# A hybrid decoder block on one core: every tile that TensorE reads begins at the same address modulo 256 bytes

## The chip, the cores and the metric

One core of one Trainium2 chip runs the whole block in one program. The metric is the device time of one execution in microseconds (us). The core has TensorE (PE), which multiplies a stationary tile of up to 128 x 128, loaded ahead as weights, by a moving tile of up to 512 columns; VectorE (DVE), ScalarE (ACT) and GpSimd (POOL) for the elementwise work; and SyncE (SP), which issues most of the DMAs. SBUF holds the tiles, as one line of bytes in each of 128 partitions. An address here is the byte in that line at which a tile begins, and its class is that address modulo 256.

## The reference

1024 tokens of 1024 features in float32; 256 memory tokens.

```python
h = rmsnorm(x, g_mix_norm)
proj = jnp.einsum('bsd,de->bse', h, w_in)
sb_q, sb_k, sb_v, fx_q, fx_k, fx_v, f_logit, m_q, gate_logit = split_columns(proj, SPLITS)
o_sb = stick_breaking_attention(...)      # 8 heads of 64, strictly causal
o_fox = forgetting_attention(...)         # 8 heads of 64, causal softmax with decay
o_mem = memory_attention(...)             # 4 heads of 128 over 256 memory tokens
gates = jax.nn.sigmoid(gate_logit.reshape(b, s, N_BRANCH, D_MODEL))
merged = gates[:, :, 0] * br_sb + gates[:, :, 1] * br_fox + gates[:, :, 2] * br_mem
x = x + jnp.einsum('bsd,de->bse', merged, w_out)
h2 = rmsnorm(x, g_mlp_norm)
u = jax.nn.relu(jnp.einsum('bsd,df->bsf', h2, w_ff_up))      # 1024 -> 4096
x = x + jnp.einsum('bsf,fd->bsd', u * u, w_ff_down)          # 4096 -> 1024
```

Each `br_` is one attention's output times its 512 x 1024 branch matrix.

## The kernel before, in words

**Precision.** A float32 operand is split into a high and a low half in the type fp32r: ACT copies the raw tile into the high half, and DVE subtracts this from the raw tile into the low half (L1056 and L1057, L141 and L142, L1976 and L1977). A product is three matmuls into one PSUM bank: high by high, high by low, low by high. The function `mm3` (L145, matmuls at L149 to L151) shows it; other stages write the same three out (L1146, L1458, L1983, L2225, L2663). The large products of 1024 x 1024 and up are made as seven half-size products of sums and differences (P1 to P7) in place of eight.

**Stages**, in us of the profiled span: norms and transposes of the tokens (L467), value and key projections and the memory's (L1146) up to 116; the query and key projections in seven products (L1458) up to 485, whose middle, 195 to 365, has the tokens stationary and 256 columns of weights moving, and whose rest has the weights stationary and 512 columns of tokens moving; attention (transposes L919, scores L936, sums and outputs L825 to L872) up to 880, with the gates and two of the three branches (L1146) laid between; more of L1146 up to 921; the last branch (`last_branch`, L149 to L151) up to 966; the output projection (L2225) up to 1049; the MLP up (L1983) up to 1366; the MLP down (L2663) to the end.

**Order.** From the start to the end of attention, and again in the MLP up, a small planner in the kernel lays down the order of each engine from costs and due times. The last branch and what follows it are written as plain loops, and there the tile framework puts the instructions of each engine in order, from its model of when tiles come free.

**Memory.** A pool gives each tag so many buffers, and the framework places pools from the left, or with side="right" from the right end. Tiles of one tag take its buffers in turn; a new tile waits until the old one's readers are done.
- `C` (L85): small statistics tiles (`st`, 27 of 32 bytes), `sm`, the identity `ident` for transposes, `fn`.
- `W` (L308): two `raw` tiles and three pairs `whi`, `wlo` for weights in float32 and fp32r, of WS = 4 x 264 floats, so 4224 bytes each, which is 16.5 times 256: neighbours alternate between two classes. `load_w` (L132) and the planner (`WP`, `RAW`, L356 and L357) take them, and `wtile` and `right_tiles` (L1863, L1866) reuse them as right-hand operands of the output projection.
- Right side: `EDGE` (L303), a pad of 24 floats, then `RA` (the transposed tokens `hTh`, `hTl`, later `x`), `E`, `MT`, and later `RB`.
- Left working tiles behind `W`: `R`, `N`, then `A` (L1608: `h`, `v`, `e`, `r` and the mask `later`), `A2` (`pth`, `ptl`, `ob`, `es`, `o`), in the MLP `M` (`raw`, `oh`, `ol`, `cu`), in the last branch `G` (`gt`, `tmp`).

**The last branch** takes four column groups of weights `ws[d2]`. Some are loaded ahead, the others in the loop by `load_w`, each with two gates rows `gt` of 128 x 1024; it also splits the right operand of the first product P1 of the output projection (`right_tiles("P1")`, at d2 == 3). Per half-row: three matmuls for each k into a bank, then DVE multiplies by the gate into `tmp` and adds it to `g`, and for the first halves ACT and DVE make the high and low half (`oh`, `ol`).

Of the kernel before, what the change touches and what calls it, by code (L numbers as in the profile page):

```python
# [14 lines left out]
F32 = mybir.dt.float32  # L15
F32R = mybir.dt.float32r
I32 = mybir.dt.int32
AF = mybir.ActivationFunctionType
# [3 lines left out]
P = 128  # L22
# [9 lines left out]
WS = 4 * 264  # L32
# [11 lines left out]
def tile_hybrid_block(  # L44
# [20 lines left out]
    nc = tc.nc  # L65
# [16 lines left out]
        def close(self):  # L82
            self.cm.__exit__(None, None, None)

    C = Pool("c", st=27, ss=4)  # L85
    dram = ctx.enter_context(tc.tile_pool(name="dram", bufs=1, space=bass.MemoryType.DRAM))
    psum = ctx.enter_context(tc.tile_pool(name="ps", bufs=1, space=bass.MemoryType.PSUM))
    PSB = {"pp": 3, "sc": 2, "tr": 2, "pv": 1}
# [9 lines left out]
        return bank(ROT[flip[0] % 5])  # L98


    ident = C.p.tile([P, P], F32, tag="ident", name="ident")
    make_identity(nc, ident)
    sm = C.p.tile([P, 8], F32, tag="sm", name="sm")
    zero, one = sm[:, 0:1], sm[:, 1:2]
    nc.vector.memset(zero, 0.0)
    nc.vector.memset(one, 1.0)
# [1 line left out]
    nc.vector.memset(eps, EPS * 2.0 ** (2 / 3))  # L108

    def root_table():  # L110
        nc.scalar.activation(C.t("st", [P, 8])[:, :1], one, AF.Sqrt)
    root_table()
    o_scr = [dram.tile([512, S], F32, name=f"o_scr{b}", tag=f"o_scr{b}") for b in range(3)]
    low_scr = dram.tile([512, S], F32, name="low_scr", tag="low_scr")
# [14 lines left out]
    def stat(n, dt=F32):  # L129
        return C.t("st", [P, 8], dt)[:, :n]  # L130

    def load_w(pieces, kk, n, pool=None):  # L132

        pool = pool or W
        raw = W.t("raw", [P, WS])[:, :kk * n].rearrange("p (k n) -> p k n", n=n)
        for off, src in pieces:
            m = src.shape[1]
            nc.sync.dma_start(raw[:, :, off:off + m], src.rearrange("(k p) n -> p k n", p=P))
        hi = pool.t("whi", [P, WS], F32R)[:, :kk * n].rearrange("p (k n) -> p k n", n=n)
        lo = pool.t("wlo", [P, WS], F32R)[:, :kk * n].rearrange("p (k n) -> p k n", n=n)  # L140
        nc.scalar.activation(hi, raw, AF.Copy)  # L141
        nc.vector.tensor_tensor(lo, raw, f32(hi), ALU.subtract)  # L142
        return hi, lo
# [156 lines left out]
        yield Sleep(machine.pipe + 2.0 - machine.now)  # L300


    EDGE = Pool("edge", side="right", edge=1)  # L303
    EDGE.t("edge", [P, 24])
    RA = Pool("ra", side="right", h=4, g0=1, g1=1, g2=1, g3=1)
    E = Pool("e", side="right", sn=10)
    MT = Pool("mt", side="right", mt=4)
    W = Pool("w", raw=2, whi=3, wlo=3)  # L308
    R = Pool("r", raw=4, s1=1)
    N = Pool("n0", gb=2, xt=7, xj=1)  # L310

# [28 lines left out]
    fox_order = (2, 3, 0, 1)  # L340
    fn = C.p.tile([P, 64], F32, tag="fn", name="fn")

# [6 lines left out]
    def tiles(pool, tag, n, shape, dt=F32):  # L349
        return Places([pool.t(tag, [P, shape], dt) for _ in range(n)])  # L350

    PP, SC, TR, PV = (banks(tag) for tag in ("pp", "sc", "tr", "pv"))
    ES, OO, EL, RR, HT, PH, PL, OB, VV, BK, LATER, NONE, RQ = (Places([]) for _ in range(13))
    SN, RS, S1 = tiles(E, "sn", 10, 512), tiles(R, "raw", 4, 1024), R.t("s1", [P, 4, 256])
    XT = tiles(N, "xt", 7, D)
    WP = Places([(W.t("whi", [P, WS], F32R), W.t("wlo", [P, WS], F32R)) for _ in range(3)])  # L356
    RAW = tiles(W, "raw", 2, WS)  # L357

    def passes(a, b):
        return ((a[0], b[0]), (a[0], b[1]), (a[1], b[0]))  # L360
# [719 lines left out]
    def loader(tasks):  # L1080
        while tasks:
# [15 lines left out]
            for load in t.loads:  # L1097
                raw, first = ahead.pop(0) if ahead else (None, False)
                pair = yield Get(WP)
                _, kk, n = load  # L1100
# [498 lines left out]
    def second_part():  # L1599
        def opened(name, *tags):  # L1600
            pool = holder[name] = Pool(name, **{tag: n for _, tag, n, _, _ in tags})
            for place, tag, n, shape, dt in tags:
# [3 lines left out]
        holder["T"].close()  # L1606
        R.close()
        opened("A", (HT, "h", 12, 512, F32R), (VV, "v", 2, 2048, F32R), (EL, "e", 4, D, F32), (RR, "r", 3, D, F32),  # L1608
               (LATER, "later", 1, 544, F32))
        later = holder["later"] = LATER.free[0][:, :513]  # L1610
        halves = [RR.free.popleft() for _ in range(2)]
        RQ.put(*(t[:, i * 512:(i + 1) * 512] for t in halves for i in range(2)))
# [248 lines left out]
    left, right, ring = {}, {}, {}  # L1861

    def wtile(tag, dt):  # L1863
        return W.t(tag, [P, WS], dt)[:, :1024].rearrange("p (k n) -> p k n", k=2)

    def right_tiles(kind):  # L1866

# [5 lines left out]
    def last_branch(gpool, os_, ws):  # L1873
        b = order[2][0]
        for d2 in range(4):
# [7 lines left out]
            for dd in range(2):  # L1883
# [9 lines left out]
                if d == 7:  # L1893
                    nc.scalar.activation(C.t("st", [P, 8])[:, :1], gt[:, :1], AF.Sqrt, bias=one, scale=0.0)
                for half in range(2):
# [53 lines left out]
    for s in range(0, ST, 2):  # L1949
        t = RA.t("h", [P, 2, D])  # L1950
        xm += [t[:, 0, :], t[:, 1, :]]

    hb = {}
# [8 lines left out]
    raws, ops, pieces = {}, {}, {}  # L1962
# [48 lines left out]
    def free(what=None):  # L2011
# [6 lines left out]
        else:  # L2018
            sb[0].close()
            M.close()  # L2020
            W.close()
            RB.close()
# [675 lines left out]
        XR.close()  # L2698

    RA.close()  # L2700
    EDGE.close()
    C.close()


# [22 lines left out]
```

## Time and profile before

| what | value |
| --- | --- |
| runs of before | 1678.10, 1678.14, 1678.90 us; median 1678.14 |
| the profiled execution | 1677.32 us, of which the span of the trace is 1675.5 |
| instructions | 24,997, of which 9118 matmuls |
| DMA | 284.32 MB, mean 170 GB/s |

The span begins with the first instruction and ends with the last; the profiled execution's own time is 1.8 us more. A matmul's start is recorded, its end modelled, so that the difference of two starts is the pace, and a duration is the pace and some 0.16 us. L is the line of the kernel before, and the operands of a matmul stand as out<-moving,stationary, so that pp<-h,whi has the tile h moving and the weights' high half stationary. In its form, 128*128 is the stationary tile and 128x512 the moving one.

### The profile page before, as it was taken

How to read it: one execution, taken by the hardware profiler on the slowest of the kernel's cores; microseconds unless marked ns; L12 is line 12 of the kernel's file. 1: busy time of each engine (PE TensorE's matmuls, PEld its weight loads, DVE VectorE, ACT ScalarE, POOL GpSimd, SP SyncE). 2: the span in 40 equal slices, each digit the busy share in tenths (PEclk: the TensorE clock that was granted, in tenths of full speed). 3: DMA queues.
4: the chain of work that ended last, by engine and by line, in shares of the span. 5: the costliest groups of instructions: out<-in, count | busy, mean ns of one | idle time of the engine just before them, and what ended most of it. 6: DMA issues, size and time to landing. Idle time of an engine off the chain costs nothing.

```text
span 1675.5 us, 24997 instructions
## 1 busy us (share of the span) xinstructions
PE 1665.9 (99%) x9118; PEld 1432.9 (86%) x9118; DVE 1292.2 (77%) x2079; ACT 849.0 (51%) x1474; POOL 255.2 (15%) x440
## 2 busy tenths in 40 slices
PE   9999999999999999999999999999999999999999
PEld 9998899998888888888888887878888888888887
DVE  7967678855449888878877898987777776787875
ACT  6445555535458898876771446533233235333331
POOL 0001000000153132255400011021221120000000
PEclk9999999999999999999999999999999999999999
DMA  6445434467374455477747552144444375464532
GB/s 246 150 159 170 163 109 147 138 187 253 130 245 133 148 156 164 138 228 220 241 142 222 206 182 95 56 155 154 144 154 154 142 274 218 176 209 174 201 126 76
DMA packets 142221, 284.32 MB, mean 170 GB/s; under 512 B 16913, under 2 KB 53329, under 8 KB 142098
## 3 DMA queue, kind: packets, MB, share of 16 engines
q1 hardware_dynamic: 110562, 183.08, 32.0%
q0 software_dynamic: 31536, 99.64, 19.0%
q8 instruction: 72, 1.18, 0.3%
q14 instruction: 51, 0.42, 0.1%
HBM read 189.83 MB, written 92.83 MB: 169 GB/s over the span
## 4 chain that ended last, share of the span: by engine, by line
PE 91%; DVE 4%; ACT 1%; issue 1%; DMA 0%; DVEq 0%; ACTq 0%
PE pp L1458 11%; PE pp L1983 10%; PE pp L1146 9%; PE pp L2663 8%; PE sc L1458 7%; PE sc L1146 6%; PE sc L1983 5%; PE tr L2663 4%; PE sc L2663 4%; PE tr L919 4%; PE pv L1458 3%; PE pv L2663 3%; PE tr L1983 2%; PE sc L936 2%; PE pp L936 2%; DVE h L1919 1%
## 5 line engine op out<-in xcount | busy, mean ns | idle before, releaser
L1057 DVE TENSOR_TENSOR wlo<-raw,whi 128x1024 fp32r<-128x1024 f32 (+1 forms) x88 | 107.4, 1221 | 80.6 <-ACT whi L1056 80.2
L1056 ACT ACTIVATE whi<-raw 128x1024 fp32r<-128x1024 f32 (+1 forms) x88 | 93.2, 1059 | 79.0 <-PE pp L1458 32.7
L1983 PE MATMUL pp<-h,oh 128*128 128x512 f32 x384 | 120.6, 395 | 0.7 <-ACT cu L2068 0.6
L926 DVE TENSOR_TENSOR ptl<-tr,pth 128x512 fp32r<-128x512 f32 (+1 forms) x160 | 99.0, 627 | 24.1 <-ACT pth L924 23.3
L924 ACT ACTIVATE pth<-tr 128x512 fp32r<-128x512 f32 (+1 forms) x160 | 87.4, 557 | 34.5 <-PE sc L936 15.4
L1983 PEld LDWEIGHTS pp<-h,oh 128*128 128x128 f32 x384 | 72.1, 188 | 18.4 <-ACT cu L2068 1.5
L1375 POOL DMA_DIRECT2D raw<-w_in x32 | 24.1, 754 | 396.6 <-DVE wlo L1057 396.6
L1458 PE MATMUL pp<-h,whi 128*128 128x512 f32 x248 | 77.7, 394 | 0.0
L1146 PE MATMUL sc<-h,whi 128*128 128x512 f32 (+1 forms) x254 | 77.2, 387 | 0.0
L1983 PE MATMUL pp<-h,ol 128*128 128x512 f32 x192 | 75.8, 395 | 0.0
L1458 PE MATMUL pp<-whi,h 128*128 128x256 f32 x384 | 72.1, 283 | 0.0
L845 DVE TENSOR_TENSOR_SCAN e<-r,e 128x384 f32<-128x384 f32 (+3 forms) x64 | 66.3, 1043 | 7.0 <-ACT e L830 6.6
L1976 ACT ACTIVATE oh<-raw 128x512 fp32r<-128x512 f32 x64 | 39.4, 624 | 61.9 <-DVE raw L1919 61.9
L2663 PE MATMUL pp<-h,h 128*128 128x512 f32 x288 | 66.6, 389 | 0.0
L2663 PE MATMUL pp<-sop,sop 128*128 128x512 f32 x288 | 66.6, 389 | 0.0
L2663 PEld LDWEIGHTS pp<-h,h 128*128 128x128 f32 x288 | 54.1, 188 | 11.3
L2663 PEld LDWEIGHTS pp<-sop,sop 128*128 128x128 f32 x288 | 54.1, 188 | 11.3
L919 PE MATMUL tr<-ident,e 128*128 128x128 f32 x416 | 62.5, 273 | 0.0
L1458 PEld LDWEIGHTS pp<-whi,h 128*128 128x128 f32 x384 | 60.4, 189 | 0.0
L919 PEld LDWEIGHTS tr<-ident,e 128*128 128x128 f32 x416 | 50.6, 140 | 10.0
L1977 DVE TENSOR_TENSOR ol<-raw,oh 128x512 fp32r<-128x512 f32 x64 | 43.1, 688 | 16.8 <-ACT oh L1976 16.8
L1458 PEld LDWEIGHTS pp<-h,whi 128*128 128x128 f32 x248 | 46.7, 189 | 11.0
(562 smaller groups left out, 5193.9 us busy)
## 6 DMA issues: line engine op xcount, KB each, us to landing
ur<-s_scr SPq DMA_DIRECT2D x26, 1024.0 KB
raw<-w_in POOLq DMA_DIRECT2D x42, 512.0 KB, 5.0
raw<-w_up SPq DMA_DIRECT2D x60, 256.0 KB
s_scr<-s POOLq DMA_DIRECT2D x60, 256.0 KB, 2.6
g<-w_down SPq DMA_DIRECT2D x14, 1024.0 KB
s_scr<-cu POOLq DMA_DIRECT2D x48, 256.0 KB, 2.8
h<-sbk_scr POOLq DMA_DIRECT2D x64, 128.0 KB, 3.1
o<-gate_scr SPq DMA_DIRECT2D x32, 256.0 KB
```

Of the source, the lines that this page charges most:

```text
L845: nc.vector.tensor_tensor_scan(out=back, data0=rho[:, :u][:, ::-1], data1=back, initial=0.0 if last else beta[:, c + u:c + u + 1], op0=ALU ...
L919: nc.tensor.transpose(tr[:, jj * 256 + a * P:jj * 256 + (a + 1) * P], es[a][:, j * P:(j + 1) * P], ident)
L924: yield Op("ACT", act_time(512 - lo_c), lambda: nc.scalar.activation(ph[:, lo_c:], tr[:, lo_c:], AF.Copy))
L926: yield Op("DVE", dve_time(512 - lo_c), lambda: nc.vector.tensor_tensor(pl[:, lo_c:], tr[:, lo_c:], f32(ph[:, lo_c:]), ALU.subtract))
L936: nc.tensor.matmul(pv[0][:, c_:256], pair.v[:, j, b, :], p_[:, jj * 256 + c_:(jj + 1) * 256], start=(k == 0 and n_ == 0 and i == 0), stop= ...
L1056: yield Op("ACT", 0.03 + act_time(m), lambda: nc.scalar.activation(hi, raw, AF.Copy))
L1057: yield Op("DVE", dve_time(m), lambda: nc.vector.tensor_tensor(lo, raw, f32(hi), ALU.subtract))
L1146: nc.tensor.matmul(ps, a_, b_, start=(first and i == 0), stop=(last and i == n - 1))
L1458: nc.tensor.matmul(out_, a_, b_, start=(first and n == 0 and j == 0), stop=(last and n == 3 and j == len(todo) - 1), skip_group_check=True)
L1977: nc.vector.tensor_tensor(l_, src, f32(h_), ALU.subtract)
L1983: nc.tensor.matmul(ps, w[a_][:, k * P:(k + 1) * P], h[b_][k], start=(first and k == 0 and i == 0), stop=(last and k == 3 and i == 2), skip ...
L2663: nc.tensor.matmul(ps, a_[:, c, qs], b_[:, c, :], start=(kind in ("P1", "P2", "P7") and c == 0 and i == 0), stop=(kind in ("P2", "P4", "P3 ...
```

## The change

All tiles that TensorE reads get an address that is 224 modulo 256. The type of each instruction, its shape and its count stay.

| tiles | class before | class after |
| --- | --- | --- |
| `ident` | 128 | 224 |
| the three pairs, high / low half | 0 / 128, 128 / 0, 0 / 128 | 224 / 224 |
| `raw` tiles of `W` | 0, 128 | 96, used as operands from column 32 on: 224 |
| left working tiles (`h`, `v`, `e`, `oh`, `ol`, `cu`, ... and the MLP-down tiles `sop`, `ur`) | 0 | 224 |
| `pth`, `ptl`, `ob`, behind the mask | 128 | 224 |
| right side (`hTh`, `hTl`, `mt`, `sn`, `x`, `RB`) | 128 | 224 |

In the MLP down the operands made in the right-side tiles (`h`) are all of class 128 before, those made in the left ones (`sop`) all of class 0, and the two do not meet in one step.

- `C`: one `st` tile less (26), a `warm` tile for the table load, `sm` and `warm` ahead of `ident`.
- `W`: eight slots of their own (`SLOTS`, `ROOM`) in the order ha, ra, la, rb, hb, lb, hc, lc, of 4224, 4096 (hb, lb) and 4352 bytes (hc, lc), taken in turn by `wide`; before, three `whi`, three `wlo` and two `raw` buffers of one size. The turns go by the count of calls, so that the calls past the planner may find another slot than before.
- `EDGE` goes; `later` has 576 floats in place of 544 (its first 513 are used).

```diff
--- before.py
+++ after.py
@@ -82,7 +82,7 @@
         def close(self):
             self.cm.__exit__(None, None, None)
 
-    C = Pool("c", st=27, ss=4)
+    C = Pool("c", st=26, ss=4)
     dram = ctx.enter_context(tc.tile_pool(name="dram", bufs=1, space=bass.MemoryType.DRAM))
     psum = ctx.enter_context(tc.tile_pool(name="ps", bufs=1, space=bass.MemoryType.PSUM))
     PSB = {"pp": 3, "sc": 2, "tr": 2, "pv": 1}
@@ -98,9 +98,10 @@
         return bank(ROT[flip[0] % 5])
 
 
+    sm = C.p.tile([P, 8], F32, tag="sm", name="sm")
+    warm = C.t("st", [P, 8])
     ident = C.p.tile([P, P], F32, tag="ident", name="ident")
     make_identity(nc, ident)
-    sm = C.p.tile([P, 8], F32, tag="sm", name="sm")
     zero, one = sm[:, 0:1], sm[:, 1:2]
     nc.vector.memset(zero, 0.0)
     nc.vector.memset(one, 1.0)
@@ -108,7 +109,7 @@
     nc.vector.memset(eps, EPS * 2.0 ** (2 / 3))
 
     def root_table():
-        nc.scalar.activation(C.t("st", [P, 8])[:, :1], one, AF.Sqrt)
+        nc.scalar.activation(warm[:, :1], one, AF.Sqrt)
     root_table()
     o_scr = [dram.tile([512, S], F32, name=f"o_scr{b}", tag=f"o_scr{b}") for b in range(3)]
     low_scr = dram.tile([512, S], F32, name="low_scr", tag="low_scr")
@@ -129,15 +130,14 @@
     def stat(n, dt=F32):
         return C.t("st", [P, 8], dt)[:, :n]
 
-    def load_w(pieces, kk, n, pool=None):
-
-        pool = pool or W
-        raw = W.t("raw", [P, WS])[:, :kk * n].rearrange("p (k n) -> p k n", n=n)
+    def load_w(pieces, kk, n):
+
+        raw = wide("raw")[:, :kk * n].rearrange("p (k n) -> p k n", n=n)
         for off, src in pieces:
             m = src.shape[1]
             nc.sync.dma_start(raw[:, :, off:off + m], src.rearrange("(k p) n -> p k n", p=P))
-        hi = pool.t("whi", [P, WS], F32R)[:, :kk * n].rearrange("p (k n) -> p k n", n=n)
-        lo = pool.t("wlo", [P, WS], F32R)[:, :kk * n].rearrange("p (k n) -> p k n", n=n)
+        hi = wide("whi", F32R)[:, :kk * n].rearrange("p (k n) -> p k n", n=n)
+        lo = wide("wlo", F32R)[:, :kk * n].rearrange("p (k n) -> p k n", n=n)
         nc.scalar.activation(hi, raw, AF.Copy)
         nc.vector.tensor_tensor(lo, raw, f32(hi), ALU.subtract)
         return hi, lo
@@ -300,12 +300,18 @@
         yield Sleep(machine.pipe + 2.0 - machine.now)
 
 
-    EDGE = Pool("edge", side="right", edge=1)
-    EDGE.t("edge", [P, 24])
     RA = Pool("ra", side="right", h=4, g0=1, g1=1, g2=1, g3=1)
     E = Pool("e", side="right", sn=10)
     MT = Pool("mt", side="right", mt=4)
-    W = Pool("w", raw=2, whi=3, wlo=3)
+    SLOTS = {"whi": ("ha", "hb", "hc"), "wlo": ("la", "lb", "lc"), "raw": ("ra", "rb")}
+    ROOM = {"ha": WS, "ra": WS, "la": WS, "rb": WS, "hb": 1024, "lb": 1024, "hc": WS + 32, "lc": WS + 32}
+    W = Pool("w", **{slot: 1 for slot in ROOM})
+    taken = dict.fromkeys(SLOTS, 0)
+
+    def wide(tag, dt=F32):
+        slot = SLOTS[tag][taken[tag] % len(SLOTS[tag])]
+        taken[tag] += 1
+        return W.t(slot, [P, ROOM[slot]], dt)
     R = Pool("r", raw=4, s1=1)
     N = Pool("n0", gb=2, xt=7, xj=1)
 
@@ -353,8 +359,10 @@
     ES, OO, EL, RR, HT, PH, PL, OB, VV, BK, LATER, NONE, RQ = (Places([]) for _ in range(13))
     SN, RS, S1 = tiles(E, "sn", 10, 512), tiles(R, "raw", 4, 1024), R.t("s1", [P, 4, 256])
     XT = tiles(N, "xt", 7, D)
-    WP = Places([(W.t("whi", [P, WS], F32R), W.t("wlo", [P, WS], F32R)) for _ in range(3)])
-    RAW = tiles(W, "raw", 2, WS)
+    made_w = {tag: [] for tag in SLOTS}
+    for tag in ("whi", "raw", "wlo", "raw", "whi", "wlo", "whi", "wlo"):
+        made_w[tag].append(wide(tag, F32 if tag == "raw" else F32R))
+    WP, RAW = Places(list(zip(made_w["whi"], made_w["wlo"]))), Places(made_w["raw"])
 
     def passes(a, b):
         return ((a[0], b[0]), (a[0], b[1]), (a[1], b[0]))
@@ -1606,7 +1614,7 @@
         holder["T"].close()
         R.close()
         opened("A", (HT, "h", 12, 512, F32R), (VV, "v", 2, 2048, F32R), (EL, "e", 4, D, F32), (RR, "r", 3, D, F32),
-               (LATER, "later", 1, 544, F32))
+               (LATER, "later", 1, 576, F32))
         later = holder["later"] = LATER.free[0][:, :513]
         halves = [RR.free.popleft() for _ in range(2)]
         RQ.put(*(t[:, i * 512:(i + 1) * 512] for t in halves for i in range(2)))
@@ -1861,7 +1869,8 @@
     left, right, ring = {}, {}, {}
 
     def wtile(tag, dt):
-        return W.t(tag, [P, WS], dt)[:, :1024].rearrange("p (k n) -> p k n", k=2)
+        t = wide(tag, dt)
+        return (t[:, 32:WS] if tag == "raw" else t[:, :1024]).rearrange("p (k n) -> p k n", k=2)
 
     def right_tiles(kind):
 
@@ -2698,7 +2707,6 @@
         XR.close()
 
     RA.close()
-    EDGE.close()
     C.close()
```

On PE and POOL the instructions stand in the order of before. On ACT, DVE and SP they stand in another order in the last branch, where the weights of the third and fourth column groups now take another slot in turn.

ACT in the last branch, before: `gt` are sigmoids of the gates, `oh` high halves of the sum `g`, `whi415` the high half of the fourth weights, `whi417` that of the right operand of P1.

```order
L1892 ACTIVATE gt381_9293<-gt381_9293 128x1024
L1892 ACTIVATE gt386_9330<-gt386_9330 128x1024
L1905 ACTIVATE oh357_9269<-g0301_7470 128x512
L1905 ACTIVATE oh358_9270<-g0301_7470 128x512
L1892 ACTIVATE gt391_9368<-gt391_9368 128x1024
L1905 ACTIVATE oh359_9271<-g1302_7471 128x512
L1892 ACTIVATE gt396_9406<-gt396_9406 128x1024
L141 ACTIVATE whi415_9534<-raw414_9532 128x1024
L1905 ACTIVATE oh360_9272<-g1302_7471 128x512
L1881 ACTIVATE whi417_9538<-h355_9267 128x1024
```

And after, from the same place on: `ha401` is the high half of the third weights, `hb414` that of the fourth, `hc416` that of the right operand.

```order
L1890 ACTIVATE hc416_9534<-h354_9263 128x1024
L1914 ACTIVATE oh356_9265<-g0300_7466 128x512
L1901 ACTIVATE gt390_9364<-gt390_9364 128x1024
L1914 ACTIVATE oh357_9266<-g0300_7466 128x512
L141 ACTIVATE ha401_9442<-ra400_9440 128x1024
L141 ACTIVATE hb414_9530<-rb413_9528 128x1024
L1901 ACTIVATE gt395_9402<-gt395_9402 128x1024
L1914 ACTIVATE oh358_9267<-g1301_7467 128x512
L1914 ACTIVATE oh359_9268<-g1301_7467 128x512
L1901 ACTIVATE gt403_9446<-gt403_9446 128x1024
```

The right operand's split has moved ahead of the weights, and the third and fourth weights' splits follow each other, ahead of the next gates.

DVE in the last branch, before, in its place 1320 to 1331: `tmp` is bank by gate, `g` the sum, `ol` a low half, `wlo416` the low half of the fourth weights.

```order
L1919 TENSOR_TENSOR g0301_7470<-g0301_7470,tmp390_9365 128x512
L1919 TENSOR_TENSOR tmp393_9385<-pp392_9372,gt391_9368 128x512
L1919 TENSOR_TENSOR g1302_7471<-g1302_7471,tmp393_9385 128x512
L1919 TENSOR_TENSOR tmp395_9403<-sc394_9390,gt391_9368 128x512
L1919 TENSOR_TENSOR ol363_9275<-g1302_7471,oh359_9271 128x512
L1919 TENSOR_TENSOR g1302_7471<-g1302_7471,tmp395_9403 128x512
L1919 TENSOR_TENSOR tmp398_9423<-pp397_9410,gt396_9406 128x512
L1919 TENSOR_TENSOR g1302_7471<-g1302_7471,tmp398_9423 128x512
L1919 TENSOR_TENSOR tmp400_9441<-sc399_9428,gt396_9406 128x512
L1919 TENSOR_TENSOR ol364_9276<-g1302_7471,oh360_9272 128x512
L1919 TENSOR_TENSOR g1302_7471<-g1302_7471,tmp400_9441 128x512
L142 TENSOR_TENSOR wlo416_9535<-raw414_9532,whi415_9534 128x1024
```

And after, in the same places 1320 to 1331: `la402` and `lb415` are the low halves of the third and fourth weights.

```order
L1928 TENSOR_TENSOR g0300_7466<-g0300_7466,tmp389_9361 128x512
L142 TENSOR_TENSOR la402_9443<-ra400_9440,ha401_9442 128x1024
L1928 TENSOR_TENSOR tmp392_9381<-pp391_9368,gt390_9364 128x512
L142 TENSOR_TENSOR lb415_9531<-rb413_9528,hb414_9530 128x1024
L1928 TENSOR_TENSOR g1301_7467<-g1301_7467,tmp392_9381 128x512
L1928 TENSOR_TENSOR tmp394_9399<-sc393_9386,gt390_9364 128x512
L1928 TENSOR_TENSOR g1301_7467<-g1301_7467,tmp394_9399 128x512
L1928 TENSOR_TENSOR ol362_9271<-g1301_7467,oh358_9267 128x512
L1928 TENSOR_TENSOR tmp397_9419<-pp396_9406,gt395_9402 128x512
L1928 TENSOR_TENSOR g1301_7467<-g1301_7467,tmp397_9419 128x512
L1928 TENSOR_TENSOR tmp399_9437<-sc398_9424,gt395_9402 128x512
L1928 TENSOR_TENSOR ol363_9272<-g1301_7467,oh359_9268 128x512
```

The fourth weights' low half stands nine places earlier than the corresponding row before, with the remaining products by the gates behind it.

## Prediction

> **What bounds the kernel now.** The page came first: its busy times, its granted clock, and its chain of work that ended last.
>
> ```profile
> PE 1665.9 (99%) x9118; PEld 1432.9 (86%) x9118; DVE 1292.2 (77%) x2079; ACT 849.0 (51%) x1474; POOL 255.2 (15%) x440
> ...
> PEclk9999999999999999999999999999999999999999
> ...
> PE 91%; DVE 4%; ACT 1%; issue 1%; DMA 0%; DVEq 0%; ACTq 0%
> PE pp L1458 11%; PE pp L1983 10%; PE pp L1146 9%; PE pp L2663 8%; PE sc L1458 7%; PE sc L1146 6%; PE sc L1983 5%; PE tr L2663 4%; PE sc L2663 4%; PE tr L919 4%; PE pv L1458 3%; PE pv L2663 3%; PE tr L1983 2%; PE sc L936 2%; PE pp L936 2%; DVE h L1919 1%
> ```
>
> TensorE is busy all the time, at the full clock, and is 91% of the chain. A busy PE may still hide waits, so the view of waits, PE's alone, came next:
>
> ```profile
> engine line waited for: us in total, times, longest us
> PE pv L417 <- POOL ident masks.py:199: 1.4, 1, 1.4
> PE pp L2307 <- ACT h L2282: 1.4, 1, 1.4
> PE tr L467 <- DVE xt L451: 0.9, 2, 0.6
> PE pp L1146 <- DVE wlo L1057: 0.9, 2, 0.7
> PE pp L1983 <- ACT cu L2068: 0.6, 1, 0.6
> ```
>
> These sum to 5.2 us of 1675.5. No wait is worth removing: the time is the pace of the matmuls, and the change can act only on that pace. So the question is how far one matmul starts behind another in each stage. The windows of PE alone give it for three stretches that hold nothing but products of 512 columns (L1458; L1983; L2663):
>
> ```profile
> core 0: us, PE busy (x), PEclk, DMA share, GB/s
> 368.00:460.00 92.00, 92.00 (x397) 1.00 0.60 193
> 1200.00:1350.00 150.00, 150.00 (x648) 1.00 0.41 147
> 1400.00:1650.00 250.00, 250.00 (x1103) 1.00 0.48 167
> ```
>
> A matmul's modelled end lies 0.16 us behind the start of the next, so one of each count began ahead of the window. The paces are 92.00/396 = 232.3 ns, 150.00/647 = 231.8 ns and 250.00/1102 = 226.9 ns, for the same shape. By the table of addresses, L2663 is the stage where the stationary tile, the next one and the moving tile all begin in one class modulo 256 bytes (all at 0 in one step, all at 128 in the next). In the other two the classes are mixed.
>
> A stage can differ for many reasons, so I looked for one loop in which only the class differs. The last branch (L149 to L151: hi*hi, hi*lo, lo*hi) has it. From 921 us the pair's hi half lies at 128 and its lo half at 0; from 932 us it is the other way round; the moving tile stays at 128. By line, in these two windows (ns min/median/max, and a duration is the pace plus 0.16 us):
>
> ```profile
> L149 PE MATMUL pp<-h,whi x8: 389/389/389, 924.1 to 931.8; 128*128 128x512 f32 x8
> L150 PE MATMUL pp<-h,whi x8: 396/396/396, 924.4 to 932.0; 128*128 128x512 f32 x8
> L151 PE MATMUL pp<-h,wlo x7: 397/397/397, 924.6 to 931.5; 128*128 128x512 f32 x7
> ...
> L149 PE MATMUL pp<-h,whi x8: 393/393/401, 932.5 to 940.2; 128*128 128x512 f32 x8
> L150 PE MATMUL pp<-h,whi x9: 395/395/398, 932.0 to 940.4; 128*128 128x512 f32 x9
> L151 PE MATMUL pp<-h,wlo x9: 397/398/404, 932.2 to 940.6; 128*128 128x512 f32 x9
> ```
>
> L149 takes 389 ns where it and the next weights share the moving tile's class, and 393 where they do not; L150 and L151, mixed in both windows, take 395 to 398. L2663 repeats the 389 in both classes, h at 128 and sop at 0:
>
> ```profile
> L2663 PE MATMUL pp<-h,h x288: 389/389/395, 1366.4 to 1592.1; 128*128 128x512 f32 x144
> L2663 PE MATMUL pp<-sop,sop x288: 389/389/393, 1442.6 to 1668.4; 128*128 128x512 f32 x144
> ```
>
> So equal classes give 389, mixed ones 393 to 398, and whether the shared class is 0 or 128 does not matter. That is the reason for what follows.
>
> **The change part by part.** *Products of 512 columns* all become equal (224 everywhere). Each is priced at its measured pace less 226.9 ns. Counts are those of the windows limited to one line, over the whole span (L1983, L2225, L1458, L1146 in this order):
>
> ```profile
> 0.00:1675.50 1675.50, 314.23 (x1344) 1.00 0.51 170
> ...
> 0.00:1675.50 1675.50, 79.67 (x336) 1.00 0.51 170
> ...
> 0.00:1675.50 1675.50, 360.69 (x2184) 1.00 0.51 170
> ...
> 0.00:1675.50 1675.50, 341.91 (x1632) 1.00 0.51 170
> ```
>
> - L1983: 1344 x 4.9 ns (231.8 less 226.9) = 6.6 us; at the 5.4 ns of L1458 it would be 7.3. Taken: 6.8.
> - L1458: 1344 of its 2184 are 256 wide, all between 195 and 365 us: by line, pp has 384 (the row below) and half as many with wlo, sc 256 and half, pv 128 and half, and with g 128 and half. That leaves 840 x 5.4 = 4.5 us.
> - L149 to L151: 192 x 5.7 (the mean of 0, 7, 8 and 4, 6, 9 above 389) = 1.1 us.
>
> ```profile
> L1458 PE MATMUL pp<-whi,h x384: 274/282/368, 195.2 to 365.1; 128*128 128x256 f32 x192
> ...
> L1146 PE MATMUL sc<-h,whi x254: 278/393/482, 22.4 to 918.1; 128*128 128x512 f32 x111, 128*128 128x256 f32 x16
> L1146 PE MATMUL pp<-g,whi x160: 387/393/477, 86.6 to 741.7; 128*128 128x512 f32 x160
> L1146 PE MATMUL pp<-h,whi x128: 387/394/477, 81.0 to 920.9; 128*128 128x512 f32 x128
> ```
>
> - L1146: some 890 of its 1632 are 512 wide (sc 222, pp 160 and 128, half as many each with wlo, and 125 in small groups). About 270 stand in unbroken runs, 270 x 5.4 = 1.4 us. The other 620 are strewn in threes among the transposes and narrow products of attention (485 to 860 us), where an equal pace may not settle: between 0 and 3.3 us, taken at 1.7.
> - L2225: 336 x 5 = 1.7 us of TensorE time, but there DVE is the limit, as the windows show:
>
> ```profile
> 945.00:970.00 25.00, 25.00 (x110) 20.24 (x109) 21.40 (x33) 12.21 (x16) 0.00 (x0) 1.00 0.36 114
> 970.00:1000.00 30.00, 30.00 (x131) 24.32 (x130) 30.00 (x43) 9.85 (x20) 7.81 (x4) 1.00 0.40 154
> 1000.00:1030.00 30.00, 28.55 (x131) 22.67 (x130) 29.25 (x54) 19.80 (x37) 0.00 (x0) 1.00 0.42 138
> ```
>
> DVE (third) has no free moment from 970 us, and PE's 1.45 us of idle in the last row are the wait of L2307. A faster TensorE only waits longer there: 0.3 us taken of 0 to 1.7.
> - L2663 is equal already: 0.
>
> Sum of the gains: 6.8 + 4.5 + 1.1 + 1.4 + 1.7 + 0.3 = 15.8 us.
>
> *Products of 256 columns* (1344 in L1458, some 1100 elsewhere) may lose. In L1458 they are mixed now; the only run of equal ones is at 700.4 us (L149 to L151, h on h):
>
> ```profile
> 343.11:365.17 22.06, 22.06 (x186) 1.00 0.51 152
> ...
> 700.39 0.28 PE L149 MATMUL pv<-h,h 128*128 128x256 f32 x1
> ...
> 701.48 0.40 PE L1146 MATMUL sc<-h,whi 128*128 128x512 f32 x1
> ```
>
> Mixed: 22.06/186 = 118.6 ns. Equal: nine matmuls in 1.09 us, about 120 ns. So equal classes cost 1.0 to 1.4 ns here: 2450 matmuls, 2.5 us lost, taken; bounds 0 (nine matmuls are few) and 3.4. Seen with the 512s (226.9 = 213.3 + 13.6, and 120 = 106.7 + 13.3, at 2.4 columns a ns, an estimate from the two paces' difference of 106.9 ns for 256 columns), equal classes give one fixed extra of 13.5 ns, while mixed ones wander: less than that at 256 columns, more at 512.
>
> *The 264-wide products, transposes and the 128-wide ones* get 0: the first still step 32 bytes from slice to slice, and transposes run on ident, whose class equals the token tiles' already.
>
> *The order* on PE is unchanged, instruction for instruction. On ACT, DVE and SP the last branch is rearranged, since the third weight pair in turn is now another slot. DVE gets lb<-rb,hb early, and it cannot run until PE has left that slot, which is where the second weights end:
>
> ```profile
> 943.88 0.69 DVE L1919 TENSOR_TENSOR tmp<-sc,gt 128x512 f32<-128x512 f32 x1 [1.33 <-PE sc L151]
> ...
> 945.69 1.22 DVE L142 TENSOR_TENSOR wlo<-raw,whi 128x1024 fp32r<-128x1024 f32 x1
> ```
>
> The slot is free at 943.4 (L151's last of the second weights). Behind the waiting split on DVE are the four evictions of groups five to eight (tmp, g and ol rows); behind its ACT half, the sigmoid of the gates of the fourth group of columns. DVE would stand from about 937.5 to 944.4 and end its split at 945.6, with nine rows of 0.61 us still to do that it now has done by 945.7, and two of 1.2 us done ahead: 3.1 us behind. PE waits only if a bank is not empty: the bank read at 946.9 is wanted about 949.2 (five groups of 2.78 us on). So the cover is 2.3 us; each us beyond it is a us of PE. The lag then meets DVE's free time of 25.00 less 21.40 = 3.6 us in the row 945:970. Taken: 0.5 us lost, bounds 0 and 3.1. The raw tiles' shift, the wider mask tile and the row strides add no instruction: 0.
>
> **Sum.** 15.8 - 2.5 - 0.5 = 12.8 us off the profiled execution's 1677.3: 1664.5. The median of the runs is 0.8 higher, so 1665.3. Runs of before lie between 1678.1 and 1678.9; about 0.2% (3.4 us) is what a measurement can tell from no change.
>
> **Rivals.**
>
> *The phase itself costs (slower).* 0 and 128 are multiples of 64 bytes; 224 is not, and no row shows an equal run there. If a start 32 bytes off such a line costs each stream one more pause (the step between 389 and 395 to 396, 6 to 7 ns), the mixed stages stay, the equal ones lose: 1344 matmuls of L2663 x 6 = 8.1 us, so 1678.1 + 8 = 1686. It decides if the 389 of L2663 becomes 395. Against it: the 264-wide slices of L1146, which begin at every multiple of 32, take no more than their eight extra columns.
>
> ```profile
> L1146 PE MATMUL pp<-whi,mt x128: 274/282/364, 92.2 to 116.1; 128*128 128x256 f32 x128
> L1146 PE MATMUL pp<-whi,g x128: 274/283/367, 35.5 to 80.9; 128*128 128x256 f32 x64, 128*128 128x264 f32 x64
> ```
>
> Chance 0.13.
>
> *Addresses do not matter (no change).* Then L149's two durations come from what ran beside it, and the time is 1678, or 0.5 more for the order. For it: six-long equal runs in attention do not settle. Against it: L2663 holds 389 through 300 us with very different neighbours. Chance 0.08. [...]
>
> *DVE takes over.* The lag of the last branch is not swallowed, attention gains nothing, and the wait of L2307 grows: 3.1 + 1.7 + 0.3 less gain and the 0.9 of the second bound at 256 columns, about 6 us back: 1671. Chance 0.12, for 1671 to 1677.
>
> *More than that.* The 256-wide ones also shrink to half of 226.9, 113.4 ns: 2450 x 5.2 = 12.7 us more and no 2.5 lost, about 1650. Against it: the run at 120 ns. Chance 0.05.
>
> **How the numbers follow.** The forecast, equal paces as summed, 1658 (attention and 256s at their better bounds) to 1671, has 0.62. Faster by over 0.2% takes that, the last rival, and three quarters of DVE's: 0.76. Within 0.2%: the no-change rival and the rest of DVE's, 0.11. Slower: 0.13. The range, 1656 to 1678.5, holds the forecast, DVE's and most of the no-change case, 0.8.
>
> **What would show it.** Right: L1983 and L1458 at 389 ns median, the windows of 368 to 460 us at 227 ns a matmul, the 256s of L1458 at 120 ns and 283 ns throughout, L2663 as now, and DVE's wait of some 6 us before the lb split near 940 us without idle on PE. Wrong: any 512-wide stage that stays at 393 to 397, L2663 above 389, or a PE wait for DVE or ACT between 940 and 1030 us that is over 3 us.

## The result and the profile after

The changed kernel takes 1668.3 us (median of 6 runs, 1666.7 to 1669.3), the kernel before, beside it, 1678.1 (6 runs, 1676.9 to 1679.3): a ratio of 0.994, 95% interval 0.9928 to 0.9953, 9.8 us less where 12.8 were forecast. In the profiled executions the span falls from 1675.5 to 1667.1 us.

The lines of the changed kernel lie 8 to 9 further on: L1466 was L1458, L1992 was L1983, L2234 was L2225, L2316 was L2307, L2672 was L2663. First its page, then the view of waits, PE's alone:

```profile
PE 1654.5 (99%) x9118; PEld 1434.6 (86%) x9118; DVE 1292.5 (78%) x2079; ACT 848.9 (51%) x1474; POOL 256.3 (15%) x440
```

```profile
engine line waited for: us in total, times, longest us
PE pp L2316 <- ACT h L2291: 3.0, 1, 3.0
PE pv L425 <- POOL ident masks.py:199: 1.4, 1, 1.4
PE pp L1992 <- ACT cu L2077: 0.9, 2, 0.7
PE pv L879 <- DVE st L884: 0.7, 1, 0.7
```

TensorE still bounds the kernel, but the wait for the normed rows (L2307 before, 1.4 us) is now 3.0, and a wait in attention is new (L879). PE alone in three stretches of 512-column products (L1466, L1992, L2672):

```profile
core 0: us, PE busy (x), PEclk, DMA share, GB/s
368.00:460.00 92.00, 92.00 (x407) 1.00 0.62 194
1200.00:1340.00 140.00, 140.00 (x619) 1.00 0.44 150
1400.00:1640.00 240.00, 240.00 (x1060) 1.00 0.48 168
```

92.00/406, 140.00/618 and 240.00/1059 are 226.6, 226.5 and 226.6 ns a matmul: the two stages that ran at 232.3 and 231.8 now run at the pace of the third. By line:

```profile
L149 PE MATMUL pp<-h,hb x16: 389/389/389, 928.8 to 958.0; 128*128 128x512 f32 x16
L1992 PE MATMUL pp<-g,oh x128: 387/389/481, 1047.7 to 1332.8; 128*128 128x512 f32 x128
L1466 PE MATMUL pp<-h,ha x88: 389/389/389, 127.0 to 478.6; 128*128 128x512 f32 x88
L1466 PE MATMUL pp<-ha,h x128: 278/283/365, 193.2 to 364.7; 128*128 128x256 f32 x128
```

The 512s stand at 389 ns, the 256s at 283 (282 before).

PE's instructions stand in the same order in both kernels, so the start of one and the same matmul can be subtracted in the two traces. Where both kernels ran without a wait and at the full clock, the differences of pace sum to some 14.2 us: L1992 +6.9, L1466's 512s +4.6, L1154's 512s +2.2, L2234 +1.4, L149 to L151 +1.1, the 256s of L1466 -1.6 and of L1154 -0.5, the rest +0.1. Of these 8.4 are left at the end; the other 5.9 went into waits and what follows them: some 3.7 between 966 and 1049 us, 1.5 in attention (700 to 850) and 1.0 from 1050 to 1400, less 0.3 won at the start. The largest, in the timeline of PE, before and after:

```profile
1023.88 1.09 PE L2307 MATMUL pp<-ident,h 128*128 128x128 f32 x8 [1.35 <-ACT h L2282]
```

```profile
739.83 0.50 PE L879 MATMUL pv<-h,h 128*128 128x512 f32 x1 [0.69 <-DVE st L884]
...
1020.51 1.63 PE L2316 MATMUL pp<-ident,h 128*128 128x128 f32 x8 [2.95 <-ACT h L2291]
```

The same eight turns take 1.63 us where they took 1.09. The windows around them (after) show why:

```profile
core 0: us, PE busy (x), PEclk, DMA share, GB/s
1017.60:1020.40 2.80, 0.00 (x0) 1.00 0.87 256
1020.92:1024.30 3.38, 3.38 (x15) 0.50 0.85 308
1024.34:1027.00 2.66, 2.66 (x13) 1.00 0.01 2
```

Behind the wait the granted clock (the number behind the count) is 0.50 for 3.4 us, and 1.00 again from 1024.3. Before, it was never below 1.00 there.

### The profile page after: what moved, and what is told of

It is laid out like the page before. It is cut to its first block, busy times and chain, and to the rows that moved or that the text cites. A ratio compares the mean times of both kernels' runs of the same rounds, so it can differ in the third digit from the quotient of the medians.

```text
span 1667.1 us, 24994 instructions
## 1 busy us (share of the span) xinstructions
PE 1654.5 (99%) x9118; PEld 1434.6 (86%) x9118; DVE 1292.5 (78%) x2079; ACT 848.9 (51%) x1474; POOL 256.3 (15%) x440
## 4 chain that ended last, share of the span: by engine, by line
PE 72%; issue 14%; DVE 7%; POOL 3%; DMA 3%; ACT 1%; SPq 0%; POOLq 0%; ACTq 0%; DVEq 0%
PE pp L1466 11%; PE pp L1154 10%; PE sc L1466 7%; PE pp L2672 7%; PE sc L1154 6%; PE tr L927 4%; PE tr L2672 4%; PE sc L2672 4%; POOL s_scr L2009 3%; PE pv L1466 3%; PE pv L2672 2%; PE sc L944 2%; PE pp L944 2%; DVE h L1928 2%; DVE tmp L1928 1%
## 5 line engine op out<-in xcount | busy, mean ns | idle before, releaser
L1992 PE MATMUL pp<-h,oh 128*128 128x512 f32 x384 | 118.7, 390 | 1.2 <-ACT cu L2077 0.9
L1992 PEld LDWEIGHTS pp<-h,oh 128*128 128x128 f32 x384 | 71.9, 188 | 17.2 <-ACT cu L2077 1.7
L1992 PE MATMUL pp<-h,ol 128*128 128x512 f32 x192 | 74.9, 390 | 0.0
L2672 PE MATMUL pp<-h,h 128*128 128x512 f32 x288 | 66.6, 389 | 0.0
L2672 PE MATMUL pp<-sop,sop 128*128 128x512 f32 x288 | 66.6, 389 | 0.0
L2672 PEld LDWEIGHTS pp<-sop,sop 128*128 128x128 f32 x288 | 54.1, 188 | 11.2
L2672 PEld LDWEIGHTS pp<-h,h 128*128 128x128 f32 x288 | 54.1, 188 | 11.2
L2009 POOL DMA_DIRECT2D s_scr<-cu x48 | 26.1, 544 | 191.7 <-DVE cu L1999 183.6
L1014 POOL DMA_DIRECT2D h<-sbk_scr x64 | 33.3, 526 | 95.5 <-PE pv L151 29.5
L944 PE MATMUL sc<-pth,v 128*128 128x256 f32 (+1 forms) x170 | 47.4, 301 | 0.0
L2587 ACT ACTIVATE h<-t 128x2048 fp32r<-128x2048 f32 (+1 forms) x9 | 15.4, 1725 | 60.2 <-DVE t L1928 56.1
L1154 PE MATMUL sc<-h,hc 128*128 128x512 f32 (+1 forms) x154 | 44.8, 375 | 0.0
L1928 DVE TENSOR_TENSOR x<-x,pp 128x512 f32<-128x512 f32 x39 | 26.6, 682 | 22.8 <-PE pp L2672 22.8
L1065 DVE TENSOR_TENSOR lb<-raw,hb 128x1024 fp32r<-128x1024 f32 x20 | 24.5, 1223 | 25.6 <-ACT hb L1064 25.5
L2009 POOL DMA_DIRECT2D s_scr<-s x60 | 32.5, 542 | 71.4 <-DVE s L1928 64.8
L1992 PEld LDWEIGHTS pp<-h,ol 128*128 128x128 f32 x192 | 36.0, 188 | 8.1 <-DVE ol L1928 0.6
```

Of the source, the lines that this page charges most:

```text
L944: nc.tensor.matmul(pv[0][:, c_:256], pair.v[:, j, b, :], p_[:, jj * 256 + c_:(jj + 1) * 256], start=(k == 0 and n_ == 0 and i == 0), stop= ...
L1014: nc.gpsimd.dma_start(f32(t[k][rows_, :]), src)
L1154: nc.tensor.matmul(ps, a_, b_, start=(first and i == 0), stop=(last and i == n - 1))
L1928: nc.vector.tensor_tensor(out_, a_, b_, op)
L1992: nc.tensor.matmul(ps, w[a_][:, k * P:(k + 1) * P], h[b_][k], start=(first and k == 0 and i == 0), stop=(last and k == 3 and i == 2), skip ...
L2009: nc.gpsimd.dma_start(s_scr[r0:r0 + P, :], t)
```

## The experiments

### The classes, one pair at a time

The weight slots, the left working tiles and the right side can be moved against each other. Making the last weight slot 128 bytes narrower moves the left tiles alone; a pad at the right end moves the right side:

```diff
-    ROOM = {..., "hc": WS + 32, "lc": WS + 32}
+    ROOM = {..., "hc": WS + 32, "lc": WS}
```

```diff
+    EDGE = Pool("edge", side="right", edge=1)
+    EDGE.t("edge", [P, 8])      # or 16, 32; none in left_96
```

Every engine's instructions stay in the order of the changed kernel.

> The changed kernel with the last slot of the weights (lc) 128 bytes narrower: the left working tiles behind it begin at 96 modulo 256, the weight slots and the right side stay at 224. It undoes the alignment of the MLP up (left tiles stationary, right tiles moving) and of the last branch (weights stationary, left tiles moving), by 128 bytes, and leaves that of the query and key projections and of L1154 up to 116 us. Theory (a pace of 226.9 ns only where stationary and moving tiles share a class modulo 256): L1992 goes from 226.9 to about 232 ns, 6.9 us; L149 to L151 from 226.9 to 229 to 235, 1.1 us; L1466 stays at 226.8; L2672 too, since its own operands still share a class (96 or 224): 7 to 9 us longer than the changed kernel, about 1676. Rival (what counts is the layout as a whole, or which half-width stage a tile is in, not the pair of classes): L1992 stays, within 1.5 us of the changed kernel; or L2672 rises too.

> The kernel left_96 with a pad of 32 floats at the right end: right side and left working tiles at 96, the weight slots at 224. Theory: the MLP up is equal again, at the class 96 (226.9 ns, no matter which class), the projections (weights stationary at 224, tokens moving at 96) are not: L1466's 840 products of 512 columns 226.8 to 232.3 ns, 4.6 us, its 1344 of 256 columns 119.9 to 118.7, 1.6 us gained, L1154 up to 2 us: 3 to 6 us longer than the changed kernel, about 1672. Rival (224 is a better phase than others): L1992 and L2672 at 96 are above 227 ns.

> The kernel left_96 with a pad of 16 floats at the right end: the right side at 160, left working tiles at 96, weight slots at 224; a distance of 64 bytes in the projections and in the MLP up. Theory (any distance modulo 256 breaks the equal pace): both at 230 to 234 ns, 10 to 13 us longer than the changed kernel, about as the kernel before. Rival (only the class modulo 64 or the half of a 256-byte line counts): both at 226.9, as the changed kernel but for the last branch (1 us).

> The kernel left_96 with a pad of 8 floats at the right end: the right side at 192, left working tiles at 96, weight slots at 224; a distance of 32 bytes in the projections, 96 in the MLP up. Theory (any distance modulo 256): both at 230 to 234 ns, about 1678. Rivals: a distance of 32 is too small to matter, L1466 stays at 226.8 while L1992 is 232; or the pace grows with the distance, 32 bytes giving a quarter of the 5.4 ns that 128 bytes give.

Measured, as ratios to the kernel before (10 runs each): left_96 1678.5 us, 1.0004 (0.9995 to 1.0014); left_96_right_96 1675.0, 0.9982 (0.9973 to 0.9991); left_96_right_160 1677.7, 0.9999 (0.9989 to 1.0009); left_96_right_192 1681.1, 1.0019 (1.0010 to 1.0029). Moving one side by 128 bytes takes the whole gain away. The lines of the MLP up, the MLP down and the projections, in this order of the kernels:

```profile
L1992 PE MATMUL pp<-g,oh x128: 387/393/479, 1050.1 to 1341.5; 128*128 128x512 f32 x128
L1466 PE MATMUL sc<-h,hc x64: 389/389/389, 121.5 to 408.6; 128*128 128x512 f32 x64
L2672 PE MATMUL pp<-h,h 128*128 128x512 f32 x288 | 66.6, 389 | 0.0
```

```profile
L1994 PE MATMUL tr<-g,oh x112: 389/389/389, 1069.5 to 1358.4; 128*128 128x512 f32 x112
L1994 PE MATMUL sc<-hc,oh x32: 392/394/395, 1075.0 to 1345.8; 128*128 128x512 f32 x32
L1468 PE MATMUL sc<-h,hc x64: 390/392/404, 121.9 to 409.8; 128*128 128x512 f32 x64
```

```profile
L1994 PE MATMUL tr<-g,oh x112: 388/392/394, 1069.3 to 1360.2; 128*128 128x512 f32 x112
L1468 PE MATMUL sc<-h,hc x64: 393/394/398, 121.2 to 408.5; 128*128 128x512 f32 x64
```

```profile
L1994 PE MATMUL sc<-h,oh x128: 392/396/399, 1090.3 to 1368.8; 128*128 128x512 f32 x128
L1468 PE MATMUL sc<-h,hc x64: 395/396/396, 121.1 to 407.8; 128*128 128x512 f32 x64
L1468 PE MATMUL pp<-ha,h x128: 277/280/364, 194.7 to 363.3; 128*128 128x256 f32 x128
```

In left_96 the MLP up leaves 389, and the MLP down and the larger part of the projections keep it. In left_96_right_96 most of the MLP up keeps it and the projections leave it, and within one line the products whose moving tile stands in a weight slot (sc<-hc,oh, moving at 224, stationary at 96) have 394 beside 389. Taken apart by the addresses of each matmul (512 columns, neighbours of the same width), every group of equal class in the large stages has a mean pace of 226.7 to 227.6 ns, at 96, 160, 192 and 224 alike; at a distance of 32, 96 or 128 bytes the groups have 232.4 to 233.5, at 64 bytes 233.3 with the stationary tile ahead of the moving one, and 229.1 with it behind (L1994 of left_96_right_160). (Single matmuls of over 300 ns are left out.) So in these groups a distance of 32 bytes is as bad as 128, the price does not grow with it, and the phase does not matter.

A product's own classes do not decide alone, however; what runs beside it counts too. In the kernel before, 127 products of L1983 and 183 of L2225 have the stationary, the next and the moving tile all at 0, but stand among others whose moving tile is at 128: they have a mean of 231.1 and 231.5 ns. The 227 held for the groups of equal class in long runs of 512-column products.

left_96 was 2 us slower than expected for two reasons that its addresses show: the sums of tokens in the projections (358 of L1466's 512s) and the left operands of L2234 stand on the left too, and went to 233.1 and 232.4 ns; L149 to L151, whose moving tiles are on the right, did not change (226.3 to 227.0). left_96_right_96 and left_96_right_192 were some 3 us slower than expected as well. In the first, the last branch and the output projection stand unequal (232.1 to 232.6 and 233.0 ns), for which its expectation has no term; in the second, the unequal products of the large stages have 233.1 to 233.5 ns, where those of the kernel before had 231.8 to 232.3.

### The order and the clock

order_kept exchanges the turns of the slots behind the planner, so that the third and fourth weights take the places of the kernel before. keep_warm puts work into the wait; order_warm does both.

```diff
+    SLOTS.update(whi=("ha", "hc", "hb"), wlo=("la", "lc", "lb"), raw=("rb", "ra"))
```

```diff
             def turns():
+                for _ in range(20 if (s, k4) == (0, 0) else 0):
+                    nc.tensor.transpose(tr[:, :P], ident, ident)
```

> The changed kernel once more, beside the three that follow, so that they are compared on one chip. Both theories: 10 us (8 to 12) less than the kernel before; in the trace a wait of about 3 us ahead of the first turns of the normed rows (L2316) and a granted clock of 0.50 for some 2 us behind it.

> The changed kernel with the turns of the weight slots exchanged behind attention (whi: a, c, b; wlo likewise; raw: b, a), so that the third and fourth weights take the slots of the kernel before, and the rows of ACT and DVE stand nearly as they stood there. Theory (the order costs): the two waits of DVE in the last branch, 2.2 us for the right operand's high half and 1.2 us for the fourth weights' high half, go; DVE is 4 to 4.6 us ahead of the kernel before at 970 us in place of 3.35; the wait at L2316 falls from 2.95 us to under 2.3, the clock stays at 1.0 behind it, and the span is 1.0 to 2.6 us shorter than that of the changed kernel. Rival (DVE has simply no more to give: its work from 942 us on is the bound whatever the order): DVE is 3.3 us ahead as now, the wait and the half clock stay, the span is within 0.5 us.

> The changed kernel with 20 more transposes of the identity (109 ns each, 2.2 us) ahead of the first turn of the normed rows, in its own bank, which the turn then overwrites: work that lies in the wait of 2.95 us. Theory (the half clock is the answer to some 3 us without a matmul): idle falls to under 1.2 us, the clock stays at 1.0, the turns and products behind take 110 and 227 to 233 ns in place of 213 and 426, and the span is 1.2 to 2.0 us shorter. Rival (the half clock comes at this place from something else, load or time): 0.50 stays, and the span is the same or up to 0.5 us longer.

> Both edits together, the exchanged slots and the 20 transposes. If the order costs and the half clock too: the wait that is left is under 0.5 us beside the transposes, and the span is 1.5 to 3 us shorter than the changed kernel's, no more than order_kept where that alone keeps the clock at 1.0. If the order costs nothing: the same as keep_warm within 0.5 us. If the transposes then reach beyond the end of the wait, up to 0.5 us longer than order_kept.

Medians of 5 runs on one chip, with their range: after_again 1667.94 (1667.39 to 1668.64; ratio to before 0.994, 0.9928 to 0.9952), order_kept 1666.71 (1665.79 to 1668.37; 0.9933, 0.992 to 0.9945), keep_warm 1666.83 (1666.38 to 1667.50; 0.9934, 0.992 to 0.9947), order_warm 1665.64 (1665.19 to 1666.69; 0.9927, 0.9915 to 0.994). The intervals overlap; the runs of order_warm and after_again do not.

keep_warm is plain. Its windows (columns as above), and its wait in the timeline:

```profile
1016.60:1020.00 3.40, 2.63 (x24) 1.00 0.80 226
1020.00:1024.00 4.00, 4.00 (x25) 1.00 0.71 268
```

```profile
1019.72 1.09 PE L2318 MATMUL pp<-ident,h 128*128 128x128 f32 x8 [0.77 <-ACT h L2291]
```

The idle time is 0.77 us, the clock stays at 1.00, the eight turns take 1.09 us, and the median falls by 1.1, just under the 1.2 to 2.0 expected. The starts say what the half clock costs: from the first of the eight turns on, PE's lead on the kernel before falls within 6 us from 3.4 to 2.1 us in the changed kernel, by 1.3 in order_kept and 1.1 in after_again, and by nothing in keep_warm. So the half clock is the answer to the wait, not to the place.

order_kept gave its 1.2 us, but not as expected. The last branch in the timeline of DVE, of the changed kernel and of order_kept (idle before a row in brackets):

```profile
929.86 1.23 DVE L1928 TENSOR_TENSOR lc<-h,hc 128x1024 fp32r<-128x1024 f32 x1 [2.23 <-ACT hc L1890]
...
940.75 1.23 DVE L142 TENSOR_TENSOR lb<-rb,hb 128x1024 fp32r<-128x1024 f32 x1 [1.19 <-ACT hb L141]
...
967.41 1.22 DVE L1928 TENSOR_TENSOR lb<-h,hb 128x1024 fp32r<-128x1024 f32 x1
```

```profile
939.19 1.23 DVE L1930 TENSOR_TENSOR lb<-h,hb 128x1024 fp32r<-128x1024 f32 x1 [3.52 <-ACT hb L1892]
...
964.68 1.22 DVE L1930 TENSOR_TENSOR lc<-h,hc 128x1024 fp32r<-128x1024 f32 x1
```

```profile
1017.79 1.13 PE L2318 MATMUL pp<-ident,h 128*128 128x128 f32 x8 [2.66 <-ACT h L2293]
```

Two waits became one of 3.52 us, later. The last split of the branch ends 2.7 us earlier than in the changed kernel; 1.5 of these PE was ahead already at 921 us (in this execution attention had no wait), so 1.2 are the order's. The other traces agree: from 921 to 972 us DVE's rows gain 1.1 us on those of the kernel before in all four with the exchanged turns (order_kept, order_warm, order_warm_again, best), and lose 0.1 to 0.2 in all four without (the changed kernel, after_again, keep_warm, shift_256). The medians of 5 runs say the same, 1.2, but their ranges overlap. But PE gains by it too (its wait of 0.6 us at 974 us is gone), and the wait at L2318 falls only to 2.66 us, with the clock at half behind it. Both theories were half right: the order costs 1.2 us of DVE, and DVE stays the bound of the stage.

### The narrow products, and the best version

All in equal classes, the 256s lose (118.6 to 119.9 ns) where the 512s gain. shift_256 sets their weights 32 bytes off where the slot has room:

```diff
+                at = 8 if u not in ("sbk", "sbq", *GATES) and pair[0].shape[-1] > 1024 else 0
+                halves_ = tuple(w_[:, at:at + 1024] for w_ in pair)
```

> The changed kernel, but the weights of the units with 256 columns moving stand 32 bytes further into their slot where the slot has room (two of three): 912 of the 1344 products of 256 columns in L1466 have their moving tile at 0, the tokens stationary at 224. Nothing else moves. Theory (equal classes cost the narrow products what they give the wide ones; at this distance left_96_right_192 had 117.7 ns): the 912 go from 119.9 to about 117.7 ns, the stretch of 116 to 485 us is 2.0 us shorter, the median about 1666. Rival (the 119.9 of the narrow products has another cause, for instance the load of the weights beside them): no change within 0.5 us.

> order_warm with the shift of shift_256. Theory: the three gains add up, since they lie in different stretches: 1.2 (order), 1.1 (clock) and 2.0 (shift) less than the changed kernel, 1663.6. Rival: what the projections give is lost to the waits in attention or at L2316, as 1 to 2 us of the change's own gain were: 1665 to 1666.

> order_warm once more as the mark for best on the same chip: 2.3 us less than the changed kernel, 1665.6, by its first runs.

```profile
L1468 PE MATMUL pp<-ha,h x128: 277/280/366, 193.1 to 362.1; 128*128 128x256 f32 x128
L1468 PE MATMUL pp<-hb,h x128: 280/283/364, 216.6 to 332.5; 128*128 128x256 f32 x128
```

The shifted ones (ha) go to 280 ns, by mean pace from 119.9 to 117.2, the others (hb) stay at 283: 912 x 2.7 ns = 2.4 us. Medians of 5 runs on one chip: shift_256 1665.35 (1664.34 to 1668.68; 0.9929, 0.9917 to 0.9942), best 1664.01 (1663.30 to 1664.57; 0.9918, 0.9905 to 0.9932), order_warm_again 1666.23 (1665.72 to 1666.88; 0.9932, 0.992 to 0.9944). The runs of best lie under all of order_warm's. On its own chip best is 13.5 us faster than the kernel before, where the changed kernel was 9.8 and 10.3 on others: the version that beats both, by some 3 to 4 us. What is left in its waits:

```profile
PE tr L475 <- DVE xt L459: 1.8, 1, 1.8
PE pv L425 <- POOL ident masks.py:199: 1.4, 1, 1.4
PE pp L1996 <- ACT cu L2081: 0.9, 2, 0.7
PE pv L879 <- DVE st L884: 0.8, 1, 0.8
```

shift_256 also holds something about the clock. Its wait at L2318 is 3.0 us, as long as the changed kernel's, and the clock stays full:

```profile
1014.00:1017.10 3.10, 0.19 (x1) 1.00 0.76 216
1017.10:1020.50 3.40, 3.34 (x21) 1.00 0.92 343
```

left_96_right_160, on the other hand, has the half clock behind a shorter wait:

```profile
1023.20:1025.10 1.90, 0.09 (x1) 1.00 0.80 229
1025.60:1028.90 3.30, 3.30 (x15) 0.50 0.82 304
```

left_96 waits 1.94 us there, and the clock stays at 1.00 as well. So length alone does not decide it. The trace's records of the granted clock show a beat: in the changed kernel it changes at 7.15, 1020.91, 1024.32 and 1666.03 us, and these lie 297, 1 and 188 times 3.413 us apart; in the kernel before at 6.69 and 1675.80 us, 489 times that apart. The half clock of after_again, order_kept and left_96_right_160 lasts 3.4 us too. Where the beat falls on the program differs from execution to execution: the half clock begins at 1020.91 us in the changed kernel and at 1019.88 in after_again, the same kernel. Laid over the waits, stretches of 3.413 us, counted from each trace's own changes, hold all 2.95 us of the changed kernel's wait and all 1.88 us of left_96_right_160's. The clock of shift_256 does not change near its wait; counted on from afar, which makes it the author's estimate, the stretches cut that wait into 1.47 and 1.50 us, and leave at most 1.33 of left_96's in one stretch. Idle times of 1.88, 2.49 (order_kept), 2.62 (after_again) and 2.95 us within one stretch were followed by the half clock; the 1.33 of the kernel before were not, nor, by that estimate, the 1.50 and 1.33.

## Why the prediction was right, and where it failed

**The pace by classes** was right, and to the size: L1983 6.9 us for 6.8, L1458 4.6 for 4.5, L149 to L151 1.1 for 1.1. It was shown by moving one side at a time: equal classes give 227 ns in unbroken runs, any others tried 229 to 233.5. That 224 is no worse than 0 or 128 is shown too (226.6 ns in L2672, 226.9 in L2663 before), so the rival of the phase is out. So is the rival of addresses that do not matter: 227 against 233 ns hang on where the two tiles begin. Whether it is the load of the weights that the moving tile meets, no run here shows. The fixed 13.5 ns of a shared class are the prediction's estimate, from the paces of 226.9 and 120 ns; why a shared class should cost a fixed time and other distances wander was not settled.

**The narrow products** cost 2.1 us (L1458 1.6, L1146 0.5) of 2.5 taken. The price came from nine matmuls at 120 ns and held for 1321: 119.9. The transposes gained nothing, as forecast, but not for the reason given: by the addresses, 416 of the 576 of L919 have their token tile at 0 and ident at 128 before, and their pace is 109.3 ns before and 109.6 after.

**L1146** gave 2.2 of 3.1. Its products have equal classes now and a mean of 229 ns (230 in attention), not 227: between the transposes and narrow products of attention 176 of 420 (those with neighbours of the same width) have 228 ns or less and 213 have 231 or more, as the prediction feared.

**The output projection** is the step that failed. It took 0.3 us of gain, with 0 as the worst, because "a faster TensorE only waits longer there". The traces show 2.4 us lost from 966 to 1049 us, and two terms were missing. The first is the order's: DVE's free time of 3.6 us did take the lag in, so that no wait stands on PE in the last branch, but DVE entered the output projection with 3.35 us on the kernel before where PE had 4.6, and order_kept shows 1.2 us of that as the order's price (0.5 taken). From there to 1024 us DVE's rows stand 3.35 to 3.38 us ahead, without a free moment up to 1000 us (DVE is the third pair below), while PE ran up to 5.0 ahead and had to give it back: 1.6 us more wait.

```profile
core 0: us, PE busy (x) PEld busy (x) DVE busy (x) ACT busy (x) POOL busy (x), PEclk, DMA share, GB/s
966.50:1000.00 33.50, 32.94 (x146) 26.94 (x145) 33.50 (x49) 11.52 (x23) 8.31 (x4) 1.00 0.41 149
```

The second was unforeseen: the longer wait halved the clock for 3.4 us, 1.1 us by keep_warm's median and 1.3 by the starts of the changed kernel's trace. A lower bound of nothing for waiting longer was wrong, since a wait can cost what comes after it. The rival of DVE taking over had the place right and lacked this term; what happened lies between it and the forecast.

**Attention** lost another 1.5 us that the prediction did not have, 1.3 of it between 736 and 744 us, about a wait of PE for DVE at 740. The order of PE and DVE there is that of before. Such waits stood in most of the executions profiled here, in those of left_96_right_96 and left_96_right_192 too (0.9 and 0.7 us), which up to there are 1.0 us behind and only 0.8 us ahead of the kernel before, and not in that of order_kept, which is as fast as the changed kernel. So it is not simply that PE comes earlier; what decides stays open.

**The check list**: the 389s and 283s came as said; DVE's wait before the fourth weights' split was 1.2 us and that before the right operand's 2.2, not 6 in one place, since PE freed the slot earlier than reckoned; and the wait on PE just under 3 us, set as the mark of being wrong, was the sign of the loss.

## What to carry to other kernels

Where TensorE is busy throughout, compare the pace of equal shapes stage by stage, and look at the addresses modulo 256 bytes of stationary and moving tiles: here a few bytes of layout were worth 5 ns for each wide product (231.8 and 232.3 to 226.6), and cost 1 to 3 ns for each product of half the width (119.9 beside 118.6 and 117.2). A faster bound engine arrives early at every other engine's rows; price each such meeting with the slack of the one it waits for, and reckon with the half clock, 1.1 us here: it followed waits of 1.88, 2.66, 2.95 and 2.97 us, though not those of 1.94 and 2.97 in two other runs. Work put into a wait that could not be shortened cost nothing here, and bought 1.1 us.

## What the runs showed of the hardware that was not expected

- A distance of 32 bytes modulo 256 broke the equal pace of 226.8 ns as fully as one of 128 (233.3 and 232.5 to 233.2 ns in L1466); the one distance that did so by halves, 229.1 ns, was a stationary tile 64 bytes behind the moving one.
- The narrow products of L1468 were faster unequal: 117.2 ns with the moving tile 32 bytes ahead of the stationary one (shift_256), 119.9 in equal classes (the changed kernel), 118.6 in the mix of the kernel before (117.5 for those among them whose stationary, next and moving tile share a class).
- A wait of 1.88 us (left_96_right_160) was followed by 3.4 us at a granted clock of 0.50, one of 2.97 us (shift_256) was not: the half clock went with the idle time within one stretch of 3.413 us, 1.88 us and more where it came, and 1.33 us in the kernel before, 1.50 by the author's estimate in shift_256, where it did not.
